# Turning the gated rows of two feed-forwards with transposing DMAs in 16-bit halves instead of TensorE transposes

## The chip, the core and the metric

The kernel runs on one core of one Trainium2 chip. The metric is device time in microseconds (us), lower is better. The engines are called by the names of the profile: PE is TensorE (matmul), PEld its weight loads, DVE is VectorE, ACT is ScalarE, POOL is GpSimd, SP is SyncE, which issues most DMAs. ACT also has a DMA queue of its own (ACTq).

## The reference, cut to what matters

One decoder layer on 256 tokens of width 2048, in 32-bit floats. The change touches its two SwiGLU feed-forwards, the first and the last stage of the layer:

```
D_MODEL = 2048;  SEQ = 256;  D_FF = 5632

def swiglu(x, w_gate, w_up, w_down):
    return (jax.nn.silu(x @ w_gate) * (x @ w_up)) @ w_down

h = h + 0.5 * swiglu(rmsnorm(h, g_ffn1), w1_gate, w1_up, w1_down)
...   # spatial gating and windowed attention, then cross-attention
h = h + 0.5 * swiglu(rmsnorm(h, g_ffn2), w2_gate, w2_up, w2_down)
return rmsnorm(h, g_final)
```

## The kernel before, in words

**Arithmetic.** Every float operand of a large matmul is held as a rounded high part and a low part that is the rest. `split` (L145 to L147) makes them: ACT copies the value into the high part (L146), DVE subtracts the high part from the value (L147). A product is three matmuls: high x high, low x high, high x low.

**Chunks and kinds.** Weights come in chunks of 1 MB (128 partitions x 4 x 512), one DMA on SP's queue each (`load`, L310 to L345). A chunk is worked as a block product of 2x2 blocks, by one of four schemes. Kind "N" is the plain one with 8 block products, 24 matmuls. "C" also has 24, on other sums of the activations. "S" is a Strassen scheme with 7 products, 21 matmuls; it needs four sums of weight blocks, which DVE adds up (L319, L322, L323) and which are split like the weights. "D" names an activation pair that serves an "S" chunk and holds what a "C" needs as well. The raw weights have three buffers, their high and low parts two each, and the split sums of "S" one each.

**Units of a feed-forward.** `ffn` first runs 11 gate/up units c = 0 to 10; each takes 8 chunks (the 2048 inner rows in steps of 256) and makes 512 columns of gate and 512 of up. In the first feed-forward unit 0 is all "N"; otherwise units 2 to 9 are "SCSCSCSC", the others "CCSCSCSC". At the end of a unit DVE joins the products (`seven_late`, L564 to L571), ACT takes the silu of the gate (L671), DVE multiplies it with up (L675 in the first feed-forward, L677 in the second). This leaves gated rows: two tiles, one for each block of 128 tokens, of 128 tokens x 512 columns. Then four down units go over the 5632 gated columns in 22 steps of 256.

**The step that is changed.** The down product needs the gated values turned, with the columns on the partitions. `rows_done(c, rows_)` (L655) does that. It adds a generator to a list of side work. That generator is resumed from within the matmul stream: `run` (L407) calls `side_step` after every six matmuls, and the generator yields 5 such steps, then 2. At each of its two resumptions (q = 0, 1) `transposed` (L225 to L231) issues four PE transposes of 128x128 into one PSUM bank, and ACT copies the bank to one half of the tile `a` in SBUF (L665), which is entered into `acts`. The profile shows the transposes as matmuls of L230 on f1a and f2a. Later `inner` (L681) takes `acts[i]`, splits it and makes the sums that its kind needs (`fill`, L201).

**What sets the order.** PE's instructions run in the order of the program text. The other engines' order is made by a planner, which knows dependencies and estimates of durations and, among instructions that are ready, prefers what stands earlier in the program; the order it finds is then fixed, and each engine runs its list in that order. The text is emitted chunk by chunk: `push` (L476) emits the load and split of a chunk, then `turn` (L468) emits the matmuls of the chunk before it and what follows on them (`flush`, where the end of a unit is marked as of high priority), and then whatever in the list `later` is due:

```
        flush()
        pending.append((run, post))
        for n, f in [x for x in later if x[0] == 0]:
            f()
        later[:] = [(n - 1, f) for n, f in later if n]
```

An entry (0, f) that the end of a unit puts there is emitted in that very turn, after the load of the next unit's first chunk and ahead of that of its second; an entry (2, f) two turns later, after the load of the third chunk.

**Tiles.** `m4` tiles are 128 x 1024 floats, from a pool of 12; `s2` tiles are 128 x 512 floats, from a pool of 6, used for the gated rows and for scratch.

Of the kernel before, what the change touches and what calls it, by code (L numbers as in the profile page):

```python
# [7 lines left out]

F32 = mybir.dt.float32
F32R = mybir.dt.float32r  # L10
AF = mybir.ActivationFunctionType
ALU = mybir.AluOpType
AX = mybir.AxisListType

P = 128
T = 256
TB = 2
# [15 lines left out]
def layer_kernel(  # L33
# [22 lines left out]
    nc = tc.nc  # L56
# [13 lines left out]
    def nm(s):  # L70
        uid[0] += 1
        return f"{s}_{uid[0]}"

    def m4(s):
        return mid.tile([P, 1024], F32, tag="m4", name=nm(s))

    def s2(s):
        return tmp.tile([P, 512], F32, tag="s2", name=nm(s))

    def bank(s):  # L80
        return trp.tile([P, 512], F32, tag="tr", name=nm(s))
# [8 lines left out]
    def silu_table():  # L90
        t = tiny.tile([P, 1], F32, tag="warmed", name=nm("warmed"))
        return nc.scalar.activation(t, ones[:, :1], AF.Silu)

# [24 lines left out]
    h = const.tile([P, TB, D], F32, name="h")  # L118
# [15 lines left out]
    def square_into(parts_ap, src, width):  # L134
        junk = s2("junk")
        nc.scalar.activation(junk[:, :width], src, AF.Square, accum_out=parts_ap)

    def split_scaled(hi, lo, src, g):

        nc.scalar.activation(hi, src, AF.Copy, scale=g)  # L140
        nc.vector.scalar_tensor_tensor(
# [27 lines left out]
    def form(s):  # L169
        return [fp.tile([P, 4, P], F32R, tag=t, name=nm(s + t)) for t in ("fh", "fl")]  # L170

    class Pair:
        def __init__(self, s, kind, base=None):
            self.kind = kind
            self.base = base or form(s)
            if kind in "SD":
                self.sums = form(s)
                if kind == "D":
                    self.more = [
                        const.tile([P, 2, P], F32R, tag="more" + t, name=nm(s + "more")) for t in "hl"  # L180
                    ]
# [40 lines left out]
    def laid(kind, k, tb):  # L222
        return BASE[kind].index(f"A{tb + 1}{k + 1}")

    def transposed(s, kind, src):  # L225

        ps = bank(s).rearrange("p (k t) -> p k t", k=4)
        for k in range(2):
            for tb in range(TB):
                nc.tensor.transpose(ps[:, laid(kind, k, tb), :], src(tb, k), ident)  # L230
        return ps  # L231

    def row_tile(kind, v, k):

        return v[:, k::2, :] if kind == "C" else v[:, 2 * k:2 * k + 2, :]

    def pair_from_rows(s, kind, src, gcol):
# [4 lines left out]
        for k in range(2):  # L242
# [4 lines left out]
            else:  # L247
                nc.scalar.activation(row_tile(kind, raw, k), row_tile(kind, ps, k), AF.Copy, scale=g)
        if kind != "N":
# [60 lines left out]
    def load(s, w, kind, pieces, between):  # L310

        raw = stream.tile([P, 4, 512], F32, tag="raw", name=nm(s + "w"), bufs=3)
        wh = stream.tile([P, 4, 512], F32R, tag="wh", name=nm(s + "wh"))
        wl = stream.tile([P, 4, 512], F32R, tag="wl", name=nm(s + "wl"))
        b = {name: (wh[:, i, :], wl[:, i, :]) for name, i in SLOT.items()}
        if kind == "S":
# [9 lines left out]
            for i, names in enumerate((("T1", "T3"), ("T2", "T4"))):  # L326
                th, tl = [
                    stream.tile([P, 2, 512], F32R, tag=f"{n}{i}", name=nm(s + n), bufs=1)
                    for n in ("th", "tl")
# [93 lines left out]
    def side_add(gen):  # L423
        side.append([now[0], gen])
# [33 lines left out]
    later = []  # L458
# [55 lines left out]
    def narrow_unit(s, w, pairs, late, beside):  # L514

        ps = []
        for c in range(2):
            raw = stream.tile([P, 8, 256], F32, tag="raw", name=nm(s + "w"), bufs=3)
            wh = stream.tile([P, 8, 256], F32R, tag="wh", name=nm(s + "wh"))
            wl = stream.tile([P, 8, 256], F32R, tag="wl", name=nm(s + "wl"))  # L520
# [33 lines left out]
    KINDS_D = "NNSNSNSN" + "NSNSNSN" + "NNSNSNN"  # L554
# [41 lines left out]
    def adds(s, c, j0, on_block=None):  # L596
# [10 lines left out]
        def early(u):  # L607
            p1, v, z = s2(s + "p1"), s2(s + "v"), s2(s + "z")
            nc.scalar.activation(p1, u["P1"], AF.Copy, scale=c)
            nc.vector.scalar_tensor_tensor(  # L610
# [40 lines left out]
    def ffn(s, get, rs, wgu, wd, on_block, first=None, on_token_block=None):  # L651
        acts = [None] * 22
        pairs = [None] * 22

        def rows_done(c, rows_):  # L655
            a = m4(s + "a").rearrange("p (q k t) -> p q k t", q=2, k=4)

            def work():
                for q in range(2):
                    yield 5 if q == 0 else 2  # L660
                    ps = transposed(
                        s + "a", KINDS_D[2 * c + q],
                        lambda tb, k: rows_[tb][:, (2 * q + k) * P:(2 * q + k + 1) * P],
                    )
                    nc.scalar.copy(a[:, q], ps)  # L665
                    acts[2 * c + q] = a[:, q]

            side_add(work())

        def gated(up, sg, r, tb):  # L670
            nc.scalar.activation(  # L671
                sg[1], sg[0], AF.Silu, scale=1.0 if r is None else r[:, tb:tb + 1]
            )
# [13 lines left out]
        def gu_unit(c):  # L687
            got = {}

            def late(u):  # L690
                r = rs()
                c22 = s2(s + "u")
                at = {(0, 0): got["p1"], (1, 1): c22, (0, 1): got["v"], (1, 0): got["z"]}
                seven_late(u, got, lambda tb, j: at[tb, j])
                gated(at[0, 1], (at[0, 0], at[0, 0]), r, 0)
                gated(c22, (at[1, 0], at[1, 0]), r, 1)
                rows_done(c, (at[0, 0], at[1, 0]))

            kinds = MORE if 2 <= c <= 9 else FEWER
            order = range(8)  # L700
            if c == (first is not None):
                order = ORDER[first is None]
            u = Unit(s + "g", "".join(kinds[j] for j in order))
            for i in range(8):
                push(
                    u, i, wgu[order[i], c], lambda j=order[i]: get(j),
                    lambda i=i: (
                        i == u.kinds.rindex("S") and seven_early(u, got), i == 7 and late(u)
                    ),
                    beside=lambda i: (  # L710
                        first[2](8 + i) if first is not None and c == 1
                        else rs() if (c, i) == (0, 5) else inner(i - 5) if c == 10 and i >= 5 else None
                    ),
                )

        def plain_gu_unit(c):
            pairs_, before, prep, rs0 = first
            u = Unit(s + "g", "N" * 8, alone=(7,))
            u.gate_first = True

            def late():
                r = rs0()
                sg = [s2(s + "sg") for _ in range(TB)]
                for tb, (g, up) in enumerate((("P2", "Q3"), ("Q4", "R"))):
                    gated(u[up], (u[g], sg[tb]), r, tb)
                rows_done(c, sg)

            pieces = {0: (1, 0, 3, 2), 1: (1, 3, 0, 2)}
            for i in range(8):
                push(  # L730
                    u, i, wgu[i, c], lambda i=i: have(pairs_, i), late if i == 7 else None,
                    pieces=pieces.get(i), beside=prep, before=before,
                )
# [747 lines left out]
```

## Time and profile before

| | |
|---|---|
| median of three runs | 2049.44 us (2048.94 to 2049.57) |
| profiled execution, first to last instruction | 2047.2 us |
| PE busy | 2034.8 us |
| DVE busy | 1859.5 us |
| ACT busy | 1225.4 us |
| DMA moved | 402.21 MB |

The profile is of one execution. A row of the groups reads: line, engine, operation, written tile <- read tiles, shape, count | busy us in all, mean ns of one | idle us of the engine before it, and what ended that idle time. A row of a timeline reads: start, duration, engine, line, operation, tiles, count, and in brackets the idle time before it with what ended it. Tile names begin with the stage: f1g and f2g are gate/up of the first and the second feed-forward, f1d and f2d down, f1a and f2a the turned gated values; w is the raw weights, wh and wl their parts, t, th and tl the sums of "S" and their parts; gp and gz are the two tiles that end as gated rows. Matmuls overlap, so the duration of one is longer than the pitch from one to the next.

### The profile page before, as it was taken

To read this page: it belongs to the slowest core of one execution; us is meant where nothing else is said; L and a number is where in the kernel's file an instruction comes from. 1 tells how busy PE (TensorE), PEld (TensorE's weight loads), DVE (VectorE), ACT (ScalarE), POOL (GpSimd) and SP (SyncE) were. 2 spreads that over 40 slices of the span, in tenths; PEclk is the share of its full clock that TensorE was granted. 3 is DMA by queue.
4 is the path that set the end of the run, shared out by engine and by line. 5 is a ranking of instruction groups with operands and counts; after the bars stand their busy time and mean duration, and the time that the engine had idled before them with its cause. 6 is when DMAs were issued, how large, how long until landed. Compare 5 with 4: busy or idle time off the path is not lost.

```text
span 2047.2 us, 24505 instructions
## 1 busy us (share of the span) xinstructions
PE 2034.8 (99%) x9411; PEld 1690.0 (83%) x9411; DVE 1859.5 (91%) x1998; ACT 1225.4 (60%) x1344; POOL 36.6 (2%) x57
## 2 busy tenths in 40 slices
PE   9999999999999999999999999999999999999998
PEld 7888888888888888888888888888888888888886
DVE  6999999999998978988988977899999999999988
ACT  7755555565555766655556665675555556565554
POOL 0000000000000110100000000000000000000000
PEclk9999999999999999999999999999999999999999
DMA  8555555555555565545545544455455555555563
GB/s 312 182 207 204 206 206 185 205 209 192 203 204 203 188 241 178 195 162 185 202 169 186 204 150 155 171 195 214 185 206 202 205 193 206 202 203 209 185 224 126
DMA packets 60421, 402.21 MB, mean 196 GB/s; under 512 B 6912, under 2 KB 8976, under 8 KB 13200
## 3 DMA queue, kind: packets, MB, share of 16 engines
q1 hardware_dynamic: 57856, 393.50, 53.0%
q0 software_dynamic: 2016, 6.30, 0.9%
q8 instruction: 74, 1.21, 0.2%
q10 hardware_dynamic: 432, 0.84, 0.1%
q14 instruction: 43, 0.35, 0.1%
HBM read 398.52 MB, written 2.10 MB: 196 GB/s over the span
## 4 chain that ended last, share of the span: by engine, by line
PE 97%; DVE 1%; ACT 1%; issue 0%; DMA 0%; POOL 0%; POOLq 0%; DVEq 0%; SPq 0%
PE f1gQ L410 16%; PE f2gQ L410 15%; PE f2dQ L410 6%; PE f1dQ L410 6%; PE f1gP L410 6%; PE f2gP L410 6%; PE xqQ L410 3%; PE f2dP L410 3%; PE f1dP L410 3%; PE woQ L410 2%; PE xoQ L410 2%; PE f2dR L410 2%; PE f1dR L410 2%; PE vQ L410 2%; PE mv0Q L410 2%; PE mv1Q L410 2%
## 5 line engine op out<-in xcount | busy, mean ns | idle before, releaser
L147 DVE TENSOR_TENSOR f1gwl<-f1gw,f1gwh 128x1536 fp32r<-128x1536 f32 (+2 forms) x94 | 181.7, 1935 | 19.8 <-ACT f1gwh L146 16.0
L146 ACT CAST f2gwh<-f2gw 128x1536 fp32r<-128x1536 f32 (+1 forms) x88 | 150.7, 1712 | 69.0 <-PE f2gQ L410 45.5
L146 ACT CAST f1gwh<-f1gw 128x1536 fp32r<-128x1536 f32 (+2 forms) x94 | 153.0, 1629 | 59.9 <-PE f1gQ L410 39.0
L147 DVE TENSOR_TENSOR f2gwl<-f2gw,f2gwh 128x1536 fp32r<-128x1536 f32 (+1 forms) x88 | 179.4, 2039 | 9.5 <-ACT f2gwh L146 7.8
L146 ACT CAST f2gth<-f2gt 128x1024 fp32r<-128x1024 f32 x82 | 84.9, 1050 | 75.9 <-DVE f2gt L319 28.8
L146 ACT CAST f1gth<-f1gt 128x1024 fp32r<-128x1024 f32 x76 | 79.0, 1051 | 76.1 <-DVE f1gt L319 30.1
L410 PE MATMUL f2gQ<-f2gwh,n4fh 128*128 128x512 f32 x317 | 124.5, 393 | 0.0
L410 PE MATMUL f2gQ<-f2gwh,n4fl 128*128 128x512 f32 x317 | 123.4, 389 | 0.0
L146 ACT CAST f2dwh<-f2dw 128x2048 fp32r<-128x2048 f32 (+1 forms) x44 | 77.3, 1757 | 61.6 <-PE f2dQ L410 39.6
L410 PE MATMUL f1gQ<-f1gwh,n1fh 128*128 128x512 f32 x286 | 112.4, 393 | 0.0
L410 PE MATMUL f1gQ<-f1gwh,n1fl 128*128 128x512 f32 x286 | 111.3, 389 | 0.0
L146 ACT CAST f1dwh<-f1dw 128x2048 fp32r<-128x2048 f32 (+1 forms) x44 | 77.3, 1758 | 56.6 <-PE f1dQ L410 38.1
L147 DVE TENSOR_TENSOR f2gtl<-f2gt,f2gth 128x1024 fp32r<-128x1024 f32 x82 | 99.6, 1220 | 8.9 <-ACT f2gth L146 8.4
L147 DVE TENSOR_TENSOR f1dwl<-f1dw,f1dwh 128x2048 fp32r<-128x2048 f32 (+1 forms) x44 | 92.1, 2093 | 12.6 <-ACT f1dwh L146 12.5
L147 DVE TENSOR_TENSOR f2dwl<-f2dw,f2dwh 128x2048 fp32r<-128x2048 f32 (+1 forms) x44 | 92.1, 2094 | 11.5 <-ACT f2dwh L146 11.3
L147 DVE TENSOR_TENSOR f1gtl<-f1gt,f1gth 128x1024 fp32r<-128x1024 f32 x76 | 92.4, 1220 | 7.7 <-ACT f1gth L146 7.2
L410 PE MATMUL f2gQ<-f2gwl,n4fh 128*128 128x512 f32 x317 | 97.6, 392 | 0.0
L410 PE MATMUL f1gQ<-f1gwl,n1fh 128*128 128x512 f32 x286 | 88.0, 393 | 0.0
L410 PEld LDWEIGHTS f2gQ<-f2gwh,n4fh 128*128 128x128 f32 x317 | 59.5, 188 | 12.3 <-DVE f2gv L569 0.4
L410 PEld LDWEIGHTS f2gQ<-f2gwh,n4fl 128*128 128x128 f32 x317 | 59.5, 188 | 11.9
L410 PE MATMUL f2gP<-f2gwh,n4fh 128*128 128x512 f32 x176 | 68.8, 391 | 0.0
L410 PEld LDWEIGHTS f2gQ<-f2gwl,n4fh 128*128 128x128 f32 x317 | 58.8, 188 | 12.0
(828 smaller groups left out, 6045.8 us busy)
## 6 DMA issues: line engine op xcount, KB each, us to landing
f2gw<-in_w_gu SPq DMA_DIRECT2D x88, 1024.0 KB, 4.8
f1gw<-in_w_gu SPq DMA_DIRECT2D x86, 1024.0 KB, 4.9
f1dw<-in_w_down SPq DMA_DIRECT2D x44, 1024.0 KB, 4.8
f2dw<-in_w_down SPq DMA_DIRECT2D x44, 1024.0 KB, 4.8
wow<-in_w_out SPq DMA_DIRECT2D x16, 1024.0 KB, 4.8
xqw<-in_w_xq SPq DMA_DIRECT2D x16, 1024.0 KB, 4.8
xow<-in_w_xo SPq DMA_DIRECT2D x16, 1024.0 KB, 4.8
qw<-in_w_in SPq DMA_DIRECT2D x8, 1024.0 KB, 4.8
```

The source lines that it names most:

```text
L146: nc.scalar.copy(hi, src)
L147: nc.vector.tensor_tensor(lo, src, hi.bitcast(F32), ALU.subtract)
L410: nc.tensor.matmul(self.banks[name], x, y, start=name not in self.begun, stop=self.left[name] == 0)
```

## The change

The gated rows are turned by DMA. A transposing DMA works on 16-bit elements here, and the values have 32 bits. So each float is taken as two 16-bit halves. `turned`, emitted at the end of the unit, does this for each block of 128 tokens: ACT copies the rows as 16-bit integers into a tile `w`, all first halves in its left part, all second halves in its right part (128 x 1024 halfwords); a transposing DMA on ACT's queue turns `w` into `t`, in eight blocks of 128 columns. `joined`, emitted two turns later, has ACT copy the turned halves back beside each other into `a`, in four copies of 128 x 512 halfwords. No PE instruction, no PSUM bank and no side step is left in this. The 11 units of both feed-forwards go through it.

```diff
         def rows_done(c, rows_):
-            a = m4(s + "a").rearrange("p (q k t) -> p q k t", q=2, k=4)
-
-            def work():
+            a = m4(s + "a")
+            words = a.bitcast(U16).rearrange("p (q i t h) -> p q i t h", q=2, i=4, h=2)
+            halves_ = []
+
+            def turned():
+                for tb in range(TB):
+                    w = s2(s + "w").bitcast(U16)
+                    nc.scalar.copy(
+                        w.rearrange("p (h c) -> p c h", h=2),
+                        rows_[tb].bitcast(U16).rearrange("p (c h) -> p c h", h=2),
+                    )
+                    t = s2(s + "t").bitcast(U16)
+                    nc.scalar.dma_start_transpose(t.rearrange("p (b r) -> p b r", b=8), w)
+                    halves_.append(t.rearrange("p (h b t) -> p b t h", h=2, b=4))
+
+            def joined():
                 for q in range(2):
-                    yield 5 if q == 0 else 2
-                    ps = transposed(
-                        s + "a", KINDS_D[2 * c + q],
-                        lambda tb, k: rows_[tb][:, (2 * q + k) * P:(2 * q + k + 1) * P],
-                    )
-                    nc.scalar.copy(a[:, q], ps)
-                    acts[2 * c + q] = a[:, q]
-
-            side_add(work())
+                    kind = KINDS_D[2 * c + q]
+                    for tb in range(TB):
+                        i, j = laid(kind, 0, tb), laid(kind, 1, tb)
+                        nc.scalar.copy(
+                            words[:, q, i:j + 1:j - i], halves_[tb][:, 2 * q:2 * q + 2]
+                        )
+                    acts[2 * c + q] = a[:, q * 512:(q + 1) * 512].rearrange(
+                        "p (k t) -> p k t", k=4
+                    )
+
+            later.append((0, turned))
+            later.append((2, joined))
```

`laid(kind, k, tb)` gives the place of a block in the order that the kind wants; `U16` is the 16-bit integer type.

More of the change, by code (lines that the diff above doesn't have):

```diff
@@ L10 @@
 F32R = mybir.dt.float32r
+U16 = mybir.dt.uint16
 AF = mybir.ActivationFunctionType
```

## The prediction

> **What bounds the kernel now.** I read the page first: its busy shares and its chain.
>
> ```profile
> span 2047.2 us, 24505 instructions
> ...
> PE   9999999999999999999999999999999999999998
> ...
> PE 97%; DVE 1%; ACT 1%; issue 0%; DMA 0%; POOL 0%; POOLq 0%; DVEq 0%; SPq 0%
> ```
>
> The profiled execution spans 2047.2 us; the median of the runs is 2049.44, so 2.2 us lie around the span, and I carry them along unchanged. The chain that ended last is TensorE for 97%. A busy PE need not be a working PE, so I read the list of what PE waited for; its first and last of five rows:
>
> ```profile
> PE xoQ L410 <- ACT n4r L248: 1.2, 1, 1.2
> ...
> PE qP L410 <- ACT qwh L146: 0.2, 1, 0.2
> ```
>
> PE waits for next to nothing. Every PE instruction taken away is therefore a gain, as long as the engines that feed PE can go faster too. That is asked stage by stage, with the windows of three gate/up units of the first feed-forward: an ordinary one of the kind "SCSCSCSC" (eight of the eleven in each feed-forward), the last one ("CCSCSCSC"), and unit 1.
>
> ```profile
> core 0: us, PE busy (x) PEld busy (x) DVE busy (x) ACT busy (x) POOL busy (x), PEclk, DMA share, GB/s
> 223.78:265.55 41.77, 41.77 (x189) 34.57 (x189) 40.05 (x38) 24.12 (x22) 0.00 (x0) 1.00 0.55 201
> 432.64:474.00 41.36, 41.36 (x188) 34.23 (x187) 38.40 (x40) 24.19 (x25) 0.59 (x2) 1.00 0.57 203
> 56.60:98.43 41.83, 41.83 (x202) 34.59 (x201) 41.64 (x54) 33.68 (x45) 0.00 (x0) 1.00 0.54 193
> ```
>
> The first number behind the window is its length, then each engine's busy time. In the ordinary unit PE is full (41.77 of 41.77), but VectorE stands at 40.05: it is 1.7 us behind PE in a unit of 41.8. In the last unit it has 3.0 us, in unit 1 only 0.2. ScalarE has 17 us free. So PE bounds, and VectorE is a second bound close underneath. Since VectorE mostly subtracts what ScalarE has just rounded (L147 after L146), a ScalarE that comes late becomes a late VectorE.
>
> **The change part by part: what PE loses.** The transposes are the matmuls of L230; the view of the tiles f1a and f2a counts them:
>
> ```profile
> L230 PE MATMUL f1a<-ident,f1gp x40: 270/272/305, 105.8 to 485.2; 128*128 128x128 f32 x40
> L230 PE MATMUL f1a<-ident,f1gz x40: 271/272/273, 105.9 to 485.3; 128*128 128x128 f32 x40
> L230 PE MATMUL f1a<-ident,f1sg x8: 270/272/273, 61.7 to 65.3; 128*128 128x128 f32 x8
> ```
>
> ```profile
> L230 PE MATMUL f2a<-ident,f2gp x44: 270/272/312, 1397.5 to 1820.4; 128*128 128x128 f32 x44
> L230 PE MATMUL f2a<-ident,f2gz x44: 271/272/273, 1397.6 to 1820.5; 128*128 128x128 f32 x44
> ```
>
> That is 176 in 44 groups of four, two groups in each of 22 stretches. Their 272 ns are not their price, because matmuls overlap. The price is read from the pitch around one group, in the timeline of PE:
>
> ```profile
> 105.07 0.39 PE L410 MATMUL f1gQ<-f1gwh,n1fl 128*128 128x512 f32 x1
> 105.30 0.62 PE L410 MATMUL f1gP<-f1gwl,n1fh 128*128 128x512 f32 x2
> 105.76 0.27 PE L230 MATMUL f1a<-ident,f1gp 128*128 128x128 f32 x1
> ...
> 106.08 0.27 PE L230 MATMUL f1a<-ident,f1gz 128*128 128x128 f32 x1
> 106.11 1.64 PE L410 MATMUL f1gQ<-f1gwl,n1fh 128*128 128x512 f32 x6
> 107.59 0.39 PE L410 MATMUL f1gP<-f1gwh,n1fh 128*128 128x512 f32 x1
> ```
>
> Ordinary matmuls start 0.23 us apart (105.07, 105.30). From 105.76 to 107.59 lie 1.83 us with six of them, 1.38 us: the group cost 0.45. So 0.90 us per unit and 44 x 0.45 = 19.8 us in all are the most that the change can give; the ordinary unit's PE need falls to 40.87 us, the last one's to 40.46. The PSUM bank that the group held goes free as well; PE waited for none, so it brings nothing.
>
> **What ScalarE gets.** Per unit, two copies out of PSUM go (L665). In come two splits of 128x1024 halfwords, two DMA issues, and four joins of 128x512. The nearest rows by elements per partition:
>
> ```profile
> L146 ACT CAST f1gth<-f1gt 128x1024 fp32r<-128x1024 f32 x76 | 79.0, 1051 | 76.1 <-DVE f1gt L319 30.1 <-PE f1gQ L410 24.3 <-DVE f1gt L323 21.7
> ...
> L146 ACT CAST f1afh<-f1a 128x512 fp32r<-128x512 f32 x22 | 13.1, 620 | 0.5 <-PE f1gQ L410 0.5
> ...
> L665 ACT COPY f1a<-f1a 128x512 f32<-128x512 f32 x22 | 12.8, 583 | 5.6 <-PE f1a L230 5.6
> ```
>
> So 2 x 1.05 + 4 x 0.62 - 2 x 0.58 = +3.4 us, an estimate, since no row has 16-bit elements or a stride of two: were each element twice as dear it would be +8, were 16 bits half the price +1.1. To this come two holds h, the time for which issuing a transposing DMA keeps ScalarE's queue. No row shows such a DMA. The ends are ScalarE's own plain issue, and the landing of a 256 KB transfer that ScalarE issued (3.2 us), as if the queue were held to the end:
>
> ```profile
> 2041.63 0.36 ACTq L1400 DMA_DIRECT2D out<-hg  x1
> ```
>
> ```profile
> q1 hardware_dynamic: 57856, 393.50, 53.0%
> ...
> f1gw<-in_w_gu SPq DMA_DIRECT2D x86, 1024.0 KB, 4.9
> ...
> h<-in_x SPq DMA_DIRECT2D x4, 512.0 KB, 10.9
> mr<-in_mem POOLq DMA_DIRECT2D x8, 256.0 KB, 5.3
> ...
> out<-hg ACTq DMA_DIRECT2D x1, 256.0 KB, 3.2
> ```
>
> Between 0.36 and 3.2 I take their geometric middle, about 1.0 us. ScalarE then has 24.1 + 3.4 + 2.0 = 29.5 us of work in 40.9: the total fits, and the question is the place. Here are ScalarE and then VectorE at the start of the ordinary unit:
>
> ```profile
> 224.62 1.47 ACT L146 CAST f1gwh<-f1gw 128x1536 fp32r<-128x1536 f32 x1
> 228.96 1.06 ACT L146 CAST f1gth<-f1gt 128x1024 fp32r<-128x1024 f32 x1 [2.87 <-DVE f1gt L319]
> 230.88 1.91 ACT L146 CAST f1gwh<-f1gw 128x2048 fp32r<-128x2048 f32 x1 [0.87 <-PE f1gQ L410]
> ...
> 241.98 1.05 ACT L146 CAST f1gth<-f1gt 128x1024 fp32r<-128x1024 f32 x1 [2.96 <-PE f1gQ L410]
> ```
>
> ```profile
> 226.43 0.69 DVE L675 TENSOR_TENSOR f1gp<-f1gv,f1gp 128x512 f32<-128x512 f32 x1
> ...
> 231.04 1.22 DVE L147 TENSOR_TENSOR f1gtl<-f1gt,f1gth 128x1024 fp32r<-128x1024 f32 x1
> 232.17 0.68 DVE L323 TENSOR_TENSOR f1gt<-f1gt,f1gw 128x512 f32<-128x512 f32 x1
> 233.18 2.29 DVE L147 TENSOR_TENSOR f1gwl<-f1gw,f1gwh 128x2048 fp32r<-128x2048 f32 x1 [0.32 <-ACT f1gwh L146]
> ...
> 243.07 1.23 DVE L147 TENSOR_TENSOR f1gtl<-f1gt,f1gth 128x1024 fp32r<-128x1024 f32 x1 [1.19 <-ACT f1gth L146]
> ```
>
> The first gated rows are ready at 227.1 (226.43 + 0.69), the second 0.6 later. The two splits and issues are emitted before the loads of the chunks that these casts belong to, so the planner will let them go first: from 227.1 they take 2.1 + 2.0 = 4.1 us, to 231.2. Behind them are queued the cast of 228.96, which then ends at 232.3, and that of 230.88, which ends at 234.2; behind each stands VectorE's subtraction, and behind that PE's next weights. VectorE can take the addition of 232.17 ahead and works until 231.7; it waits 0.6 us for the first cast, subtracts until 233.5, and waits 0.7 for the second. That is 1.3 us of waiting where 0.32 was.
>
> VectorE's unit then is 40.05 busy, 0.2 of small gaps and 1.3 of waits: 41.55. The 1.19 us at 243.07 I leave out: that cast waited for PE to free a buffer (2.96 before 241.98), and a VectorE that runs later finds the buffer free. 41.55 lies above PE's 40.87, so VectorE sets the ordinary unit, and 0.22 of the 0.90 us are gained: 16 x 0.22 = 3.5 us. In the six other stretches VectorE has room, as in the last unit (38.40 + 0.2 + 1.3 = 39.9 under 40.46), and 0.90 comes in full, but for unit 1, where 41.64 of 41.83 allows about nothing: 5 x 0.90 = 4.5 us. Each tenth of a microsecond more or less in h moves the ordinary unit by 0.2 and the sum by 3.2 us; from h = 1.25 nothing is left of the gain.
>
> **What is hidden.** The joins wait for the DMAs, with ScalarE's casts queued behind them. They are emitted two chunks later, and the first gap that holds their 2.5 us is that before 241.98. The second issue ends at 231 to 234; a landing of 5.3 us gives 237 to 239, and I price the wait at nothing. The transposes move 44 x 0.25 = 11 MB, 3% of the 393.5 MB of weights, on DMA engines 53.0% busy; a weight load (4.9 us) that shares with one may come a fraction of a microsecond later, which I take as nothing, since SP's loads are issued when VectorE frees a buffer. The four scratch tiles per unit are from a pool of six whose next user is six chunks later.
>
> The sum: 2047.2 - 3.5 - 4.5 = 2039.2, and with the 2.2 around it 2041.
>
> **The rivals.** *The full gain.* If h is near the plain issue, the block ends at 227.1 + 2.1 + 0.7 = 229.9, the cast of 228.96 is 0.9 us late and that of 230.88 hardly; VectorE's unit stays at some 40.7 and PE the bound: 19.8 less 0.7 in unit 1, 2030. For it: PE's row of waits, and ScalarE's 17 free us, into which the planner may place the block better than I do. Against: VectorE would have to be 98% busy in sixteen units.
>
> *ScalarE's queue is held for longer, and the kernel gets slower.* At h = 1.8, the arithmetic middle of the two ends, VectorE waits 1.3 + 1.6 = 2.9 us in the ordinary unit: 43.15, 1.4 over the 41.77 of now, +22; in the other stretches 38.40 + 0.2 + 2.9 is 41.5, about the 41.36 of now, and unit 1 loses some 2: 2074. It decides from the same h = 1.25, and every 0.1 beyond it costs 3.2 us. For it: the 0.32 row shows that the cast has no slack, and VectorE has 0.6 us per unit to catch up in. Against: the order that the planner found for this kernel leaves PE no waits.
>
> *The joins wait for the landing.* If the eight column blocks of a transpose go one after the other, a landing is nearer to the slowest row of the view, 10.9 us: 232 + 10.9 = 243, joins until 245.5, and the cast at 241.98 with all behind it comes 3.5 us late. VectorE's unit would be 41.55 + 3.5 = 45.0, +3.3 in sixteen units and some 2 in the others: about 2114. The Trainium skill, page "VectorE: DVE Perf Modes", sections "The three transpose paths" and "Rules for kernel authors", speaks against this change: it gives 1309 ns for a 128x128 transpose by DMA against 390 ns on TensorE and advises TensorE where PSUM will do; eight blocks at that price are an estimate of 10.5 us. The trace of before has only TensorE's side (272 ns, 0.11 in pitch). Against the rival: 256 KB land in 3.2 and 5.3 us in the rows above.
>
> **How the numbers follow.** Forecast 0.38 (h from 0.7 to 1.2, 2032 to 2048), full gain 0.18, held queue 0.34, late landing 0.10. A measurement tells 0.2%, 4 us, from no change. Faster are the full gain and three quarters of the forecast, those under 2045: 0.47. Within 4 us, 0.15: the rest of the forecast, and a held queue near its point of decision. Slower 0.38. The range goes from 2028 to 2072: the first two cases, and of the held queue about two thirds, up to nearly h = 1.8. Cases of both signs have weight here; the forecast's own range is 2032 to 2048.
>
> **What would show it.** L230 on f1a and f2a is gone, and 44 transposes on ScalarE's DMA queue stand in their place. If I am right, the ordinary unit's window is about 41.5 us, VectorE over 96% busy in it, and its longest waits are for casts at L146 soon after the unit's start. If the unit is 40.9, the issue was short. If it is over 42, ScalarE shows the issues right before the late casts (held queue), or joins that waited for a DMA (late landing). The forecast is wrong at its root if PE still sets a unit of 41.8, or if the cost sits in the weight loads.

## The result, and the profile after

The changed kernel takes **2252.2 us** (median of four runs, 2251.35 to 2252.44) against 2049.51 us for the kernel before in the same measurement: ratio 1.0988, 95% interval 1.0975 to 1.1002. That is slower by a tenth, and outside the forecast range of 2028 to 2072.

The page of the changed kernel, its span, its busy times, the rows of PE in 40 slices and the engines of its chain:

```profile
span 2250.7 us, 24260 instructions
...
PE 2088.0 (93%) x9235; PEld 1710.9 (76%) x9235; DVE 1861.8 (83%) x1998; ACT 1461.0 (65%) x1432; POOL 34.3 (2%) x57
...
PE   9988888889999999999999999999888888889998
...
PEclk9998888999999999999999999999998999889999
...
PE 75%; ACT 15%; issue 4%; DVE 3%; ACTq 2%; DMA 1%; POOL 0%; SPq 0%; POOLq 0%; DVEq 0%
```

The transposes are gone, and yet PE is busy for 53 us more than before (2088.0 against 2034.8). Many slices of the two gate/up stages have fallen from 9 to 8, and in some of them the granted clock has fallen too. ACT, 1% of the chain before, is now 15% of it. What PE waits for, the two longest rows (total us, times, longest):

```profile
PE f1gQ L411 <- ACT f1gth L147: 60.7, 16, 5.4
PE f2gQ L411 <- ACT f2gth L147: 60.4, 15, 5.5
```

In an ordinary unit these are two waits, as shown below, one of 5.4 and one of 2.4 us, both for the cast of a Strassen sum on ACT. The window of one ordinary unit, same columns as in the prediction:

```profile
264.05:315.75 51.70, 43.94 (x181) 35.20 (x180) 40.14 (x38) 34.84 (x27) 0.00 (x0) 0.90 0.53 173
```

It is 51.70 us long where it was 41.77. VectorE's work is the same as before (40.14 against 40.05), ACT's has risen by 10.7 us, and PE ran at a granted clock of 0.90. The timeline of ACT at that unit's start shows what stands ahead of the cast:

```profile
262.59 1.47 ACT L147 CAST f1gwh<-f1gw 128x1536 fp32r<-128x1536 f32 x1
263.96 4.94 ACT L664 COPY f1w<-f1gp 128x1024 uint16<-128x1024 uint16 x1
268.92 1.25 ACTq L669 DMA_TRANSPOSE f1t<-f1w  x1
270.21 4.78 ACT L664 COPY f1w<-f1gz 128x1024 uint16<-128x1024 uint16 x1 [1.32 <-DVE f1gt L323]
275.02 1.25 ACTq L669 DMA_TRANSPOSE f1t<-f1w  x1
276.31 0.67 ACT L677 COPY f1a<-f1t 128x512 uint16<-128x512 uint16 x1 [1.32 <-issue]
276.89 1.04 ACT L147 CAST f1gth<-f1gt 128x1024 fp32r<-128x1024 f32 x1
277.84 1.83 ACT L677 COPY f1a<-f1t 128x512 uint16<-128x512 uint16 x3
279.57 1.90 ACT L147 CAST f1gwh<-f1gw 128x2048 fp32r<-128x2048 f32 x1
```

The block of two splits and two issues is where the prediction put it. It runs from 263.96 to 276.3, 12.3 us, where 4.1 were forecast: each split takes 4.8 to 4.9 us, not 1.05. Right behind it come the joins, among the casts. On VectorE and then on PE:

```profile
269.24 0.68 DVE L323 TENSOR_TENSOR f1gt<-f1gt,f1gw 128x512 f32<-128x512 f32 x1
277.96 1.22 DVE L148 TENSOR_TENSOR f1gtl<-f1gt,f1gth 128x1024 fp32r<-128x1024 f32 x1 [8.05 <-ACT f1gth L147]
...
281.50 2.29 DVE L148 TENSOR_TENSOR f1gwl<-f1gw,f1gwh 128x2048 fp32r<-128x2048 f32 x1 [1.71 <-ACT f1gwh L147]
...
291.89 2.29 DVE L148 TENSOR_TENSOR f1gwl<-f1gw,f1gwh 128x2048 fp32r<-128x2048 f32 x1 [1.57 <-ACT f1gwh L147]
```

```profile
272.01 0.39 PE L411 MATMUL f1gQ<-f1gwh,n1fl 128*128 128x512 f32 x1
272.24 0.39 PE L411 MATMUL f1gQ<-f1gwl,n1fh 128*128 128x512 f32 x1
277.98 0.80 PE L411 MATMUL f1gQ<-f1gth,n1fh 128*128 128x512 f32 x1 [5.36 <-ACT f1gth L147]
...
279.00 0.63 PE L411 MATMUL f1gQ<-f1gth,n1fh 128*128 128x512 f32 x1
279.43 0.63 PE L411 MATMUL f1gQ<-f1gth,n1fl 128*128 128x512 f32 x1
...
282.47 0.79 PE L411 MATMUL f1gQ<-f1gth,n1fh 128*128 128x512 f32 x1 [2.41 <-ACT f1gth L147]
```

VectorE waits 8.05 us for the first cast, 1.71 for the second and 1.57 for a later one, which itself had waited 1.06 us for PE to free a buffer. With its 40.14 us of work that makes 51.47 of the unit's 51.70 us, so VectorE's lateness sets the unit. PE waits 5.36 and 2.41 us. After its wait PE is slower as well: the matmuls start 0.42 us apart (279.00, 279.43), where 0.23 was the pitch before it (272.01, 272.24). The granted clock was 0.50 from 277.98 to 282.47, and 1.00 again from 290.00 on.

**Where the 203.5 us are** (2250.7 - 2047.2, the two spans). The experiment e4, in which nothing is turned, has PE busy for 2016.4 us with the same 9235 matmuls: 18.4 less than before, which is what taking the transposes away is worth. The changed kernel's PE is busy for 71.6 us more than that with the same matmuls, which goes with the slower clock. PE's idle time grew from 12.4 (2047.2 - 2034.8) to 162.7 us (2250.7 - 2088.0), by 150.3. So -18.4 + 71.6 + 150.3 = 203.5. This is an account of PE's time and not of causes: with a faster clock PE would in part only have waited longer for VectorE. In the unit above PE is busy for 43.94 us, 3.1 more than an ordinary unit takes in e9 below, and of VectorE's time only the 1.57 us of its third wait can hang on that. What the slow clock costs by itself no run separates.

### The profile page after: what moved, and what is told of

It is laid out like the page before. It is cut to its first block, busy times and chain, and to the rows that moved or that the text cites. A ratio compares the mean times of both kernels' runs of the same rounds, so it can differ in the third digit from the quotient of the medians.

```text
span 2250.7 us, 24260 instructions
## 1 busy us (share of the span) xinstructions
PE 2088.0 (93%) x9235; PEld 1710.9 (76%) x9235; DVE 1861.8 (83%) x1998; ACT 1461.0 (65%) x1432; POOL 34.3 (2%) x57
## 4 chain that ended last, share of the span: by engine, by line
PE 75%; ACT 15%; issue 4%; DVE 3%; ACTq 2%; DMA 1%; POOL 0%; SPq 0%; POOLq 0%; DVEq 0%
PE f2gQ L411 10%; PE f1gQ L411 10%; PE f2dQ L411 5%; PE f1dQ L411 5%; ACT f1w L664 4%; ACT f2w L664 4%; PE f2gP L411 4%; PE f1gP L411 4%; PE xqQ L411 3%; PE f2dP L411 3%; PE f1dP L411 2%; PE woQ L411 2%; ACTq L669 2%; PE xoQ L411 2%; PE f2dR L411 2%
## 5 line engine op out<-in xcount | busy, mean ns | idle before, releaser
L411 PE MATMUL f2gQ<-f2gth,n4fh 128*128 128x512 f32 x164 | 75.3, 459 | 60.4 <-ACT f2gth L147 60.4
L411 PE MATMUL f1gQ<-f1gth,n1fh 128*128 128x512 f32 x152 | 70.4, 463 | 60.7 <-ACT f1gth L147 60.7
L411 PEld LDWEIGHTS f2gQ<-f2gth,n4fh 128*128 128x128 f32 x164 | 35.6, 217 | 76.0 <-ACT f2gth L147 68.8
L411 PEld LDWEIGHTS f1gQ<-f1gth,n1fh 128*128 128x128 f32 x152 | 33.1, 218 | 76.3 <-ACT f1gth L147 69.9
```

The source lines that it names most:

```text
L411: nc.tensor.matmul(self.banks[name], x, y, start=name not in self.begun, stop=self.left[name] == 0)
```

## The experiments

The theory after the result: the split is expensive because it writes 16-bit elements in jumps (neighbouring elements go to two places 1 KB apart), and the length of the block at the unit's start is the loss. The rivals: the hold of ACT's queue by the issue; the joins that wait for the landing; the mere presence of any such block at that place. Times are medians beside the kernel before in the same measurement, 2049.1 to 2049.9 us.

**e1: the split written in order.** Same elements, same count, same place; the copy now runs through `w` from left to right and jumps in reading instead.

```diff
-                        w.rearrange("p (h c) -> p c h", h=2),
-                        rows_[tb].bitcast(U16).rearrange("p (c h) -> p c h", h=2),
+                        w.rearrange("p (h c) -> p h c", h=2),
+                        rows_[tb].bitcast(U16).rearrange("p (c h) -> p h c", h=2),
```

> The changed kernel, with one thing different: ScalarE's split walks the halfwords so that it writes each half of the tile from left to right and reads with a stride of two, instead of reading from left to right and jumping 1 KB between any two halfwords it writes. Theory A (the scattered writing is what makes a split 4.9 us): a split takes 1.1 us, the block of two splits and two issues (1.25 us each) 4.8 us instead of 12.2, and by the prediction's own sum, whose point of no gain lies at an issue of 1.25 us, the time is 2035 to 2060. Theory B (ScalarE is slow on 16-bit elements as such): a split stays at 4.9 us and the time at 2250. Theory C (the transposing DMAs and the hold of their issue do the harm): the split may get shorter, but the time stays above 2150.

Measured: 2139.68 us (2136.5 to 2141.52), ratio 1.0444, interval 1.0427 to 1.0461. The instructions and their order on every engine are those of the changed kernel, but for the form of this copy, so 112.5 us are the price of the form alone. The row of the copy (minimum, median, maximum in ns), and two rows of what ACT waits for:

```profile
L664 ACT COPY f1w<-f1gp x10: 1037/1040/1048, 100.5 to 522.5; 128x1024 uint16<-128x1024 uint16 x10
```

```profile
ACT f1a L677 <- DMA f1t<-f1w: 36.5, 17, 4.0
...
ACT f2a L677 <- DMA f2t<-f2w: 34.3, 17, 2.7
```

The split takes 1.04 us, as theory A expected. But the time is far above the 2035 to 2060 that it gave: 90 us of loss remain, and a wait that the changed kernel hardly had is now there: joins waiting for the landing, 70.8 us in 34 times. The timeline of ACT at a unit's start in e1:

```profile
246.81 1.25 ACTq L669 DMA_TRANSPOSE f1t<-f1w  x1
248.10 0.68 ACT L677 COPY f1a<-f1t 128x512 uint16<-128x512 uint16 x1 [1.32 <-DMA f1t<-f1w]
248.69 1.04 ACT L147 CAST f1gth<-f1gt 128x1024 fp32r<-128x1024 f32 x1
...
253.58 1.25 ACT L677 COPY f1a<-f1t 128x512 uint16<-128x512 uint16 x2 [3.26 <-DMA f1t<-f1w]
254.73 1.89 ACT L147 CAST f1gwh<-f1gw 128x2048 fp32r<-128x2048 f32 x1
```

The joins stand in ACT's list straight behind the second issue, mixed with the casts. At 253.58 two of them waited 3.26 us, and the weight cast of 254.73 behind them was late; VectorE waited 5.07 us for it.

**e2: no split at all.** The rows go to the transposing DMA as they are, and the joins scale by 0.25 to keep the numbers bounded; the halves are not parted.

```diff
-                    nc.scalar.copy(w ..., rows_[tb] ...)
-                    nc.scalar.dma_start_transpose(t.rearrange("p (b r) -> p b r", b=8), w)
+                    nc.scalar.dma_start_transpose(t.rearrange("p (b r) -> p b r", b=8), rows_[tb].bitcast(U16))
```

> The splits are left out: the transposing DMAs read the gated rows as they lie, so that the halves come out mixed and the values are not the reference's; the joins scale by a quarter, so that no value overflows. Issues, landings and joins are all still there. Theory A (the splits do the harm): the block on ScalarE is 2.5 us, and 2030 to 2045 come out. Theory C (issues and landings do it): the time stays above 2150.

Measured: 2054.6 us, ratio 1.0026, interval 1.0015 to 1.0036. Without splits nearly all of the loss is gone, although the 44 issues on ACT's queue, the landings and the joins remain. The issues are therefore not the main cost. The 2030 to 2045 that were expected are not there either: joins still waited 24.8 us for landings, in 9 times.

**e3: scattered splits, no DMA.** The joins read the parted but unturned rows.

```diff
-                    t = s2(s + "t").bitcast(U16)
-                    nc.scalar.dma_start_transpose(t.rearrange("p (b r) -> p b r", b=8), w)
-                    halves_.append(t.rearrange("p (h b t) -> p b t h", h=2, b=4))
+                    halves_.append(w.rearrange("p (h b t) -> p b t h", h=2, b=4))
```

> The changed kernel with the transposing DMAs left out: scattered splits as in the change, joins read the split tile directly, so nothing is turned and the values are not the reference's. No issue, no landing. If the scattered splits alone make most of the loss: 2170 to 2230. If issue and landing are needed for it: below 2120.

Measured: 2210.12 us, ratio 1.0784, interval 1.0765 to 1.0804. With no transposing DMA in the program, 161 of the 203 us of loss are still there. So no property of the DMA, neither hold nor landing, is needed for the greater part.

**e4: nothing turned.** Two plain copies of 128x512 floats take the place of splits, issues and joins: the ceiling of what the change could bring.

```diff
+                for q in range(2):
+                    nc.scalar.copy(a[:, q * 512:(q + 1) * 512], rows_[q])
...
-            later.append((0, turned))
-            later.append((2, joined))
+            later.append((1, copied))
```

> Nothing is turned at all: no transposes on TensorE, no DMAs, ScalarE copies the gated rows as they are with two copies of 128x512 floats per unit, so the values are not the reference's. This measures what the 176 PE transposes are worth by themselves. The prediction's term: 19.8 us less, 2030, if VectorE can follow. Rival: VectorE is the bound right underneath and gives back part of it: 2035 to 2045.

Measured: 2032.76 us (2032.56 to 2032.89), ratio 0.9919, interval 0.9904 to 0.9934. The ceiling is 16.4 us; the prediction's own value for it, the full gain, was 2030.

**e5: other engines and forms.** The form of the split changes with the unit number c.

```diff
+                    form = c % 5
+                    # 0: ACT scattered, 1: ACT in order, 2: GpSimd in order, 3: VectorE in order, 4: VectorE scattered
```

> One look at the length of a split in five forms, one form per unit c, by c modulo 5: ScalarE writing scattered, ScalarE writing in order, GpSimd in order, VectorE in order, VectorE scattered. Theory A: ScalarE scattered 4.9 us, in order 1.1 us; VectorE scattered well above VectorE in order. Theory B: both ScalarE forms 4.9 us. The total is a mixture and says little: 2090 to 2160 by A, over 2200 by B.

Measured: 2180.96 us (one run), above the 2090 to 2160 of theory A, though the lengths on ACT and VectorE came out as it said. The rows of the split of one tile in the second feed-forward:

```profile
L672 ACT COPY f2w<-f2gp x2: 1036/1038/1041, 1511.1 to 1748.6; 128x1024 uint16<-128x1024 uint16 x2
L677 POOL COPY f2w<-f2gp x2: 7039/7046/7052, 1553.6 to 1795.9; 128x1024 uint16<-128x1024 uint16 x2
L682 DVE COPY f2w<-f2gp x2: 683/684/685, 1604.6 to 1846.9; 128x1024 uint16<-128x1024 uint16 x2
L687 DVE COPY f2w<-f2gp x2: 2852/2888/2925, 1649.8 to 1891.2; 128x1024 uint16<-128x1024 uint16 x2
```

VectorE pays for the jumping write as well, 2.89 us against 0.68. Two such copies in order would be 1.4 us per unit on VectorE, which has 0.8 to spare beside PE's 40.87 us, so VectorE wasn't tried for all units.

**e6: in order, and the joins later.** e1, and the joins come four turns after the unit's end and are tied behind the last cast of the chunk just loaded. The tie is there because the planner fills a gap with whatever it takes for ready, so that to emit the joins later need not move them (this alone wasn't tried).

```diff
+        last_cast[0] = nc.scalar.copy(hi, src)      # in split
...
+                with tc.issue_after(last_cast[0].ins):
+                    put_together()                      # the four joins
...
-            later.append((2, joined))
+            later.append((4, joined))
```

> The split written in order (1.04 us), and the four joins tied behind the casts of the fifth chunk in ScalarE's order, so that they cannot stand where the planner had put them, in front of a cast and ahead of the landing. Theory D (of the 90 us that the split in order still loses, most are joins that wait for the landing with casts queued behind them): no join waits for a DMA, and 2035 to 2065. Theory E (the block of splits and issues itself makes the casts late): the waits move to the casts, and the time stays above 2100.

Measured: 2052.66 us (11 runs, 2051.79 to 2054.36), ratio 1.0018, interval 1.0009 to 1.0027: 87.0 us less than e1. No join waits for a DMA any more. But the move also changed what the planner did with the other work: one weight cast now stands between the two splits, and VectorE's order is another. So the 87.0 us belong to this whole order, and how many of them to the joins alone isn't shown. What PE still waits for:

```profile
PE f1gQ L413 <- DVE f1gtl L150: 8.1, 9, 1.8
PE f2gQ L413 <- DVE f2gtl L150: 7.8, 13, 1.0
```

The longest wait is 1.8 us, and it is for VectorE. VectorE is not full itself: in the ordinary unit from 268.75 to 311.19, 42.44 us, it works for 39.85 and waits for two weight casts in the middle of the unit, far behind the block of splits and issues. Both casts had waited for PE to free a buffer (0.54 and 2.40 us):

```profile
289.45 2.29 DVE L150 TENSOR_TENSOR f1gwl<-f1gw,f1gwh 128x2048 fp32r<-128x2048 f32 x1 [1.06 <-ACT f1gwh L149]
...
299.64 2.29 DVE L150 TENSOR_TENSOR f1gwl<-f1gw,f1gwh 128x2048 fp32r<-128x2048 f32 x1 [1.42 <-ACT f1gwh L149]
```

**e7: the same, issued from SP.** `nc.sync.dma_start_transpose` in e6, so that ACT holds nothing.

> As the one with the joins tied later, but SP's queue issues the transposes, so the 2 x 1.25 us per unit no longer lie on ScalarE. If those holds still cost, this is 5 to 25 us faster than with ScalarE's issue: 2032 to 2045. Rival: SP now waits for the split and holds up weight loads behind it: slower than with ScalarE's issue, and VectorE or ScalarE wait for DMAs of weights.

Measured: 2053.64 us, ratio 1.0021, interval 1.0012 to 1.003. With ACT free of 2.5 us per unit nothing is gained. SP's weight loads did not take the gain away: ACT's casts wait for them as in e6 (8.1 us in all in the first feed-forward, 7.8 there), and VectorE's two waits in the ordinary unit are the same, 1.08 and 1.44 us. So the hold of the issue is not what keeps e6 above the ceiling, and the prediction's slope of 3.2 us for each tenth of h is not borne out.

**e8: split and joins on GpSimd, issue on SP.** e1 with `nc.gpsimd.tensor_copy` for both, `nc.sync` for the DMA, the joins five turns later.

> Split and joins on GpSimd, issue on SP: ScalarE has nothing left of the turning, and less than before the change (two copies less per unit). If ScalarE's queue was the whole cause, 2031 to 2040, near the 2032.8 of the kernel that turns nothing. Rival: GpSimd takes several microseconds per copy beside a full VectorE (one of its copies took 7.0 us, others 1.03), or slows VectorE down: 2045 or more.

Measured: 2207.93 us, ratio 1.0771, interval 1.0757 to 1.0786. What ACT waits for:

```profile
ACT f2gwh L147 <- DMA f2gw<-in_w_gu: 100.7, 10, 12.5
...
ACT f1gwh L147 <- DMA f1gw<-in_w_gu: 90.7, 15, 11.9
```

ACT's casts wait up to 12.5 us for weights. SP's list is in order: a transposing issue that waits for GpSimd's split (12.06 us in the median for the first tile of a unit in the first feed-forward, though spans on POOL are rough) holds up the weight loads behind it. SP waited for these splits 28 times, up to 20.0 us at once, 348 us in all. The step was moved away from ACT, and ACT became late by SP's queue.

**e10: the scattered split, with the joins later.** The changed kernel with the joins of e6.

> The changed kernel with its scattered splits (4.9 us each) and only the joins tied later, behind the casts of the fifth chunk. If scattered splits and joins that wait add up (113 us and 87 us, measured one after the other), 2165. If the splits alone are enough to make the casts late, and the long block had already covered the landing: 2200 to 2250, hardly faster than the change.

Measured: 2222.56 us, ratio 1.0845, interval 1.0825 to 1.0865. Against the changed kernel that is 29.6 us less, where the same move was worth 87.0 us with the split in order. The two costs do not add. In the changed kernel the joins hardly wait for landings (2.6 us in 2 times, against 70.8 in 34 in e1), which fits that the longer splits give the transposes time to land. The order of the instructions on every engine is that of e6, so e10 and e6 are a second pair that differs in the form of the split alone: with the joins out of the way this form costs 169.9 us (2222.56 against 2052.66).

**e9: everything in gaps.** e1, with each split and its issue by itself: the first behind the first cast of the next unit's fifth chunk, the second behind the second cast of its seventh, the joins behind the first cast of the first chunk of the unit after that.

```diff
-            later.append((0, turned))
-            later.append((2, joined))
+            later.append((4, lambda: behind(0, lambda: turned(0))))
+            later.append((6, lambda: behind(1, lambda: turned(1))))
+            later.append((8, lambda: behind(0, joined)))
```

`behind(k, work)` ties `work` after cast number k of the chunk just loaded.

> Split in order, and the pieces of the turning taken apart and tied in ScalarE's order: the first split with its issue behind the first cast of the next unit's fifth chunk, the second behind the second cast of its seventh chunk, the joins behind the first cast of the unit after it. There ScalarE had idle gaps of 2.4 to 3.8 us. Theory F (the 20 us that the kernel with joins tied later still loses to the one that turns nothing are casts behind the block at the unit's start; it is the place, not ScalarE's total): 2033 to 2044, faster than before the change. Rival: ScalarE's and VectorE's pace is set by the sum of what is added, wherever it stands: 2048 to 2056.

Measured: **2034.07 us** (2032.77 to 2035.54), ratio 0.9925, interval 0.9911 to 0.9939. It is faster than the kernel before by 0.75%, clear of the noise, and PE is busy for 2016.3 us, as in e4 (2016.4). An ordinary unit, and ACT's timeline around the two splits and the joins:

```profile
182.17:222.97 40.80, 40.80 (x182) 33.80 (x181) 40.04 (x38) 27.24 (x25) 0.00 (x0) 1.00 0.69 236
```

```profile
195.80 1.04 ACT L668 COPY f1w<-f1gp 128x1024 uint16<-128x1024 uint16 x1
196.87 1.25 ACTq L673 DMA_TRANSPOSE f1t<-f1w  x1
199.06 1.05 ACT L150 CAST f1gth<-f1gt 128x1024 fp32r<-128x1024 f32 x1 [2.22 <-DVE f1gt L324]
...
206.91 1.04 ACT L668 COPY f1w<-f1gz 128x1024 uint16<-128x1024 uint16 x1
207.97 1.25 ACTq L673 DMA_TRANSPOSE f1t<-f1w  x1
209.32 1.05 ACT L150 CAST f1gth<-f1gt 128x1024 fp32r<-128x1024 f32 x1 [1.38 <-DVE f1gt L328]
...
218.05 2.43 ACT L681 COPY f1a<-f1t 128x512 uint16<-128x512 uint16 x4
```

PE is full in the unit at 40.80 us (the prediction worked out 40.87 as its need), at a granted clock of 1.00, while VectorE does 40.04 of the same 40.80. At 199.06 and 209.32 the cast behind each issue is waiting for VectorE, not for the issue.

**e11: e9 issued from SP**, with `nc.sync` for the DMA.

> The same with SP's queue issuing the transposes, so that a piece on ScalarE is 1.05 us instead of 2.3. Theory F: as fast or up to 5 us faster than with ScalarE's issue, if the pieces did not quite fit their gaps. Rival: SP waits for the split with weight loads behind it, 2 to 10 us slower.

Measured: **2032.36 us** (2032.01 to 2033.67), ratio 0.9918, interval 0.9904 to 0.9931. This is the ceiling of e4 (2032.76), with everything turned, and the best version found. Its runs overlap those of e9, so whether the issue on SP is worth the 1.7 us between them isn't shown.

**e12: what a jumping write costs.** e9, with one more copy in seven of the units, whose result nobody reads: 32-bit elements in jumps of 1 KB, halfwords with a step of 4 bytes, in jumps of 128 bytes, straight, and in jumps of 1 KB both in reading and in writing.

> One look at single copies on ScalarE that nobody reads, one beside the first split of units 2 to 8, in the kernel with the pieces in the gaps: units 2 and 3, 128x512 floats with neighbouring writes 1 KB apart; 4 and 5, 128x1024 halfwords written with a step of 4 bytes; 6, halfwords with neighbouring writes 128 bytes apart, a sixteen at a time; 7, halfwords straight; 8, halfwords with reads and writes both jumping 1 KB. If any write that leaves its neighbourhood costs 4.8 ns: 2.5 us for the floats, 4.9 for units 6 and 8. If only halfwords that jump are dear: the floats 0.6, unit 4 1.05 or dear too if any gap between halfwords suffices, unit 8 4.9, unit 7 1.05. The total is not compared; it should lie within 5 us of the kernel without these copies.

Measured: 2038.88 us (one run). The rows of that copy in the first feed-forward, in this order:

```profile
L676 ACT COPY f1x<-f1gp x2: 1162/1164/1165, 156.1 to 196.9; 128x512 f32<-128x512 f32 x2
L680 ACT COPY f1x<-f1gp x2: 1361/1362/1362, 237.7 to 278.5; 128x1024 uint16<-128x1024 uint16 x2
L685 ACT COPY f1x<-f1gp x1: 4967/4967/4967, 319.3 to 319.3; 128x1024 uint16<-128x1024 uint16 x1
L690 ACT COPY f1x<-f1gp x1: 1045/1045/1045, 361.6 to 361.6; 128x1024 uint16<-128x1024 uint16 x1
L692 ACT COPY f1x<-f1gp x1: 4947/4947/4947, 402.4 to 402.4; 128x1024 uint16<-128x1024 uint16 x1
```

Straight, 1024 halfwords take 1.045 us. A step of 4 bytes makes 1.36. Any jump from one element to the next makes 4.95 to 4.97, whether by 128 bytes or by 1 KB. For 32-bit elements the jump makes 1.16 us for 512, against 0.62 straight in e4's plain copies; that lies between the two expectations (2.5 and 0.6). So it is the writing in jumps, dear above all in 16 bits; that a read jumps as well changes nothing (4.947).

## Why the prediction was wrong

**The step that failed: "2 x 1.05" for the splits.** I took the price of a copy by the number of elements, and the highest price that I tried was "each element twice as dear". Written in jumps, a split costs 4.7 times a straight one (4.95 against 1.04 in e1). The diff showed the jump (`w` is written as "p c h"); I named it a stride of two, looked for a bound in rows that all write straight, and put the whole uncertainty on the DMA. The 44 splits are 214 us of ACT's time (the rows of L664 are 4.95 and 4.77 us in the median) instead of 46. Shown by two pairs of runs, in each of which every engine has the same instructions in the same order: 112.5 us go with the form of that one copy (e1), and 169.9 with the joins out of the way (e6 against e10).

**The mechanism was right.** The block stands at the unit's start, the two casts are queued behind it, VectorE waits for them, and VectorE's lateness sets the unit. With the measured sizes the prediction's formula gives a block of 4.94 + 4.78 + 2 x 1.25 = 12.2 us from 227.1, the cast's end at 240.4, a VectorE that waits 8.7 us from 231.7 (8.05 measured) and 0.7 for the second cast, and so a unit of 40.05 + 0.2 + 9.4 = 49.65. Sixteen units lose 7.9 each and six others about 6.6 (48.0 against 41.36): 126 + 40, some 2215 us. The kernel in which no join waits, as the formula assumes, is e10, at 2222.56. That the sums are so close is in part luck: the planner ordered e10 otherwise, and in an ordinary unit there (258.45 to 308.60) VectorE waits 0.93, 4.99, 2.61 and 1.44 us and not 8.7 and 0.7. The last two are of the kind that the prediction left out ("a VectorE that runs later finds the buffer free"): casts that had waited for PE. Such waits did not go away; the changed kernel has one of 1.57 us, and e6 has 1.06 and 1.42.

**Joins "priced at nothing": wrong.** Placing them elsewhere, with the new order of casts that came with it, is worth 29.6 us in this kernel and 87.0 with a split in order. I let the planner place them in the first gap that holds them. It put them straight behind the second issue, ahead of the landing; that its estimate of the transpose is too short would explain this, but isn't shown. The landing itself was shorter in the median than I had assumed (3.3 us against 5.3), and longer at the most (6.9), so the rival of the late landing was wrong on the price of the DMA and right that a cast would stand behind a join that waits: at 253.58 in e1 the wait was 3.26 us. Moving the joins away (e6) removes it.

**The hold h: 1.25 us, forecast 1.0 between 0.36 and 3.2.** The row of the issues, and the time from issue to landing in the view of the tile f1t:

```profile
L669 ACTq DMA_TRANSPOSE f1t<-f1w x22: 1247/1248/1322, 55.6 to 583.6; - x22
...
DMA to landing us min/median/max: 3.0/3.3/6.3
```

It happens to be the break-even of the prediction's formula, and e6, the design that the formula describes, is 3.6 us above the kernel before. But this agreement is luck and no evidence for the formula's slope: e7 takes the hold off ACT and gains nothing, and in e6 VectorE does not wait behind the block at all, where the formula has its waits, but for the two casts in the middle of the unit. The rival of the held queue, which had 0.34, is refuted as the cause of the loss (e3 has no hold at all and loses 161 us); its picture, a block on ACT ahead of the casts, is what happened, by another instruction.

**What was left out altogether: the clock.** The prediction says nothing of PE's clock. After a wait of some 5 us PE runs for a while at a pitch of 0.42 instead of 0.23 us, and over the kernel PE's busy time is 71.6 us longer for the same matmuls. How much of that is lost time is open, as said above: while VectorE sets the unit, most of it need not be. The Trainium skill, page "TensorE: Matmul & The Clock Gate", section "Why this matters for your kernels", warns of gaps of PE of more than about 3 us between bursts of matmuls, after which the clock goes back to half. The traces here agree: the changed kernel, with waits of 5.4 us, has a mean granted clock of 0.952, e1, with waits up to 4.7, 0.981, e6, with waits up to 1.8, 0.998, and e9, whose longest wait in the gate/up units is 1.6 us, 0.999.

**What held.** PE's saving was forecast as 19.8 us at most, and e4 shows 18.4 in PE's busy time and 16.4 in the whole. The weight loads cost nothing: their median to landing is 4.8 us, 4.9 before. VectorE's 98% in an ordinary unit, which I held against the full gain, is reached in e9 (40.04 of 40.80).

**What stays open.** e6 and e9 differ by 18.6 us. Neither a join's wait nor the issue explains it (e6 has none of the first, e7 none of the second on ACT). In the ordinary unit (42.44 us against 40.80) the difference lies in VectorE's waits for weight casts, 1.06 and 1.42 us in e6 and 0.43 in e9. Why they arise is open: the splits and the joins stand elsewhere, but the planner's order of the other work differs too between the two kernels, on VectorE above all, and the runs don't separate these.

## What to carry to other kernels

Before pricing a copy by its element count, look at which side jumps: an access pattern that writes neighbouring elements to distant places can cost several times a straight one, and turning the loops around so that the read jumps instead may be free. Where an engine's order is fixed, place work that waits for a DMA by hand behind what must not wait, and look in the trace whether it stands there. A change that frees a full engine pays only if what it puts on the others stands in their gaps: the same splits in order, DMAs and joins gave 2139.7 us where the planner had put them (e1) and 2034.1 us in the gaps (e9).

## What the runs showed of the hardware

- Writes that jump, ACT: 128x1024 halfwords in 4.95 us against 1.04 in order, with jumps of 128 bytes and of 1 KB alike; 1.36 with a step of 4 bytes; 128x512 floats 1.16 against 0.62. VectorE: 2.89 against 0.68. Reads that jump: the joins, which read from two places 1 KB apart by turns, take 0.67 us for 512 halfwords, where 512 floats straight take 0.62; a jumping read beside a jumping write adds nothing (4.95 against 4.97). The Trainium skill, page "SBUF — State Buffer", section "Door 1: The DMA port swizzle (why `[64,N]` ≈ `[32,N]`)", says that consecutive accesses to the same line of 16 bytes run at full rate and that each access that crosses to a new line pays. The writes agree in the main: jumps out of the line are dear, and a step of 4 bytes, with which four writes share a line, stays cheap, though not quite at the full rate (1.36 against 1.04). The reads do not agree (0.67 against 0.62), and the size of the penalty is not the same for both widths.
- A transposing DMA of 128x1024 halfwords holds the queue that issues it for 1.25 us on ACT and 1.23 on SP (e11) in the median, up to 3.5 in e2, where a plain issue holds ACT's for 0.36. It lands 3.0 us after the issue at the earliest and 3.3 in the median of the changed kernel; in e9 it is 5.3 and 4.6 in the medians of the two feed-forwards and 11.9 at the most; why it is longer there isn't shown.
- GpSimd's copy of one and the same shape took between 1.03 and 12.06 us (e5, e8); its spans are rough, and why isn't settled.
